# GpSimd substitution on 16x16 blocks with a 16-to-32 step on TensorE, and grouped beta/alpha products

## The chip, the cores and the metric

One core of a Trainium2 chip runs the program. The metric is device time in microseconds (us), lower is better. The kernel before takes 2449.17 us, the median of three runs (2448.19 to 2454.17).

## The reference

Two layers of a hybrid block act on 384 tokens: 128 context tokens and 256 latent tokens, 2048 channels wide. In each layer one input projection feeds two branches. Branch A is a 31-tap depthwise convolution with a LayerNorm. Branch B is a bidirectional gated DeltaNet with 8 heads of 128 channels. For a chunk of tokens, a head and a direction it solves a unit-triangular system:

```
beta = sigmoid(beta_l)                     # 8 heads x 2 directions a token
g    = -exp(a_log) * softplus(alpha_l + dt_bias)
a    = einsum(kb, k) * decay               # kb = k * beta
a    = where(strict, a, 0.0) + eye(CHUNK)  # unit lower triangular
u    = triangular_solve(a, v * beta)
w    = triangular_solve(a, kb * exp(g))
```

`beta_l` and `alpha_l` are 32 columns of the input projection. The branches are gated, merged and projected back, and a residual is added.

## The kernel before

Activations lie channel by token: tiles of 128 channels by 384 tokens. Weights stream in halves of 8 blocks of 128x128 (512 KB, tile `w`). ScalarE rounds a half to `whi`, VectorE (for some halves GpSimd) subtracts to get `wlo`, and TensorE forms three 384-column products for each block (`mm3`, line 332): `whi` by the high part of the activation, `whi` by its low part, `wlo` by the high part. These main products write `pm`. Every tensor instruction of a kind is recorded at one helper line: products at line 148, VectorE and GpSimd arithmetic at 177, DMAs at 201, ScalarE at 137.

The order on every engine is written at build time by a planner (lines 75 to 210) that books a cost for each instruction and keeps a clock for each engine. `slot` (line 403) issues one quarter of a main job, 12 products, after which generators waiting for "p" may put small products on TensorE; generators in phase "v" put VectorE and ScalarE work ahead of the next slot. The convolution (`conv31`, `t<-px,par,t` in the rows) is filler: it goes onto VectorE until VectorE's booked clock has reached TensorE's. Engines run their queues in order.

A layer has these stages in the profiled execution. First the opening: normalised tiles `hn[k]`, k = 0 to 15, are made, and the first jobs and the beta/alpha product run (`ba_mm`, line 643: 32 weight columns by the 384 columns of a float32 tile `h`, one product for each k at column group 32*(k % 4), written to `px`). Then the head stage: 40 main jobs for q, k, v and the convolution's inputs, among which the 8 heads run as generators. Then wide main products only.

A head's `invert` (line 813) solves two directions by three blocks of 128 tokens, six systems (`NI`). From each it takes the four diagonal 32x32 blocks into `dg`, writes them to DRAM (`dd`) and reads them back as 24 partitions of 32x32 (`ax`). GpSimd inverts them by substitution: 31 steps, each an outer product into `o` and a subtraction from `ax` (lines 830 to 836). The result goes through DRAM (`dx`) into `xc`, with four DMAs where rows change partitions. VectorE spreads it to `x64` and `xt64`; TensorE then builds 64x64 and 128x128 inverses in four groups of small products (`ypf`/`ypb`, `xf`/`xb`, `y2p`, `x2p`, tiles `h`). `head_out` applies the result. `free` (line 839) holds the generator until TensorE's booked clock has reached the end booked for `dx`.

The SP queue issues the weight loads and all the DMAs named but `dx`, which is GpSimd's.

Of the kernel before, what the change touches and what calls it, by code (L numbers as in the profile page):

```python
# [52 lines left out]
for _n, _w in PAR:  # L53
# [1 line left out]
    _o += _w  # L55
NPAR = _o

CST = [("ident", 128), ("mask_f", 128), ("mask_b", 128), ("xmask", 64),
       ("ones", 128), ("sel32", 32), ("sel2", 2)]
CST_OFF = {}  # L60
_o = 0
# [7 lines left out]
def hybrid_step_kernel(ctx: ExitStack, tc: tile.TileContext, x_in, cvec, w_mod, w_modt, w_first, w_in, w_ba,  # L69
# [351 lines left out]
    def mod_job(l, cs):  # L421

        w = []

        def load(n):
            for a in ((0, 3, 6), (9, 12, 15))[n]:
                b = min(a + 3, KT)
                t = t2([P, 3, 2, P])
                dma(out=t[:, 0:b - a], in_=w_mod[cs[0]][:, a:b])
                w.append(t)  # L430

        def run():
            v = pg([P, 2, P])
            for q in range(2):
                def mms(q=q):
                    for k in range(8 * q, 8 * q + 8):
                        g = 32 * (k % 4)
                        mm_(v[g:g + 32], csil[:, k, :], w[k // 3][:, k % 3], start=(k < 4), stop=(k >= 12))
                slot(last_half[0], mms)
            live[0] -= 6  # L440
            spawn(finish(v))

        def finish(v):
            vs = t1([P, 2, P])
# [13 lines left out]
            while "v" not in rs_x:  # L458
                yield
            h = make_hn(l, k)  # L460
            live[0] += 1 - (k % 2)
            yield "p"
            ba_mm(k, h)
            hn_done.add(k)

        return {"w": w, "load": [lambda n=n: load(n) for n in range(2)], "run": run}
# [161 lines left out]
    def make_hn(l, k, lo_eng=ptt):  # L628

        if k == 0:  # L630
            if l:
                load_ba(l)
            ba["ps"] = px([P, NTOK])
        u, h = t1(), t1()
        for s, sl in ((0, CTX), (1, LAT)):
            stt(out=u[:, sl], in0=xt[k][:, sl], scalar=amul[l][:, k, s:s + 1], in1=rs_x["v"][:, sl],
                op0=ALU.mult, op1=ALU.mult)
            act(h[:, sl], u[:, sl], AF.Identity, bias=modt[l][:, k, s:s + 1])
        hn[k] = t2([P, 2, NTOK], F32R)
        split(hn[k], h, False, lo_eng)  # L640
        return h

    def ba_mm(k, h):
        g = 32 * (k % 4)
        mm_(ba["ps"][g:g + 32, :], ba["w"][:, k, :], h, start=(k < 4), stop=(k >= 12))

    gd = {}

# [164 lines left out]
    def invert(l, hd):  # L813
# [9 lines left out]
        dd = dram.tile([P, NI, 32], F32, tag="dd", name="dd", bufs=2)  # L823
        dma(out=dd, in_=dg.rearrange("p d b i -> p (d b) i"))
        yield 2
        ax = sub.tile([4 * NI, 32, 32], F32, tag="ax", name="ax", bufs=NA)
        for q in range(4):
            dma(out=ax[NI * q:NI * q + NI], in_=dd[32 * q:32 * q + 32].rearrange("j n i -> n j i"))
        pset(out=ax.rearrange("p i j -> p (i j)")[:, 0:1024:33], value=1.0)
        for j in range(31):  # L830
            n, m = 31 - j, j + 1
            o = sub.tile([4 * NI, 256], F32, tag="o", name="o", bufs=1)
            ov = o[:, 0:n * m].rearrange("p (r c) -> p r c", r=n)
            ptt(out=ov, in0=ax[:, j, j + 1:32].unsqueeze(2).to_broadcast([4 * NI, n, m]),
                                    in1=ax[:, j, 0:m].unsqueeze(1).to_broadcast([4 * NI, n, m]), op=ALU.mult)
            ptt(out=ax[:, j + 1:32, 0:m], in0=ax[:, j + 1:32, 0:m], in1=ov, op=ALU.subtract)
        dx = dram.tile([4 * NI, 32, 32], F32, tag="dx", name="dx", bufs=2)
        dma(out=dx, in_=ax, q="pool")
        free = last[0]
        while clock["pe"] < free:  # L840
# [9 lines left out]
        xc = t1([P, NI, 32])  # L850
        for q in range(4):
            dma(out=xc[32 * q:32 * q + 32], in_=dx[NI * q:NI * q + NI].rearrange("n i c -> i n c"))
        yield 2
        x64, xt64 = h1([P, NI, 64]), h1([P, NI, 64])
        tt(out=x64.rearrange("p n (e c) -> p n e c", e=2), in0=xc.unsqueeze(2).to_broadcast([P, NI, 2, 32]),
           in1=C("xmask").rearrange("p (e c) -> p e c", e=2).unsqueeze(1).to_broadcast([P, NI, 2, 32]), op=ALU.mult)
        vtrans(out=xt64.rearrange("p n (e c) -> p (n e) c", e=2), in_=x64.rearrange("p n (e c) -> p (n e) c", e=2))
        yield "p"
# [167 lines left out]
    def layer(l):  # L1026
# [244 lines left out]
            return f  # L1271


        hk = {}

        def open_layer():
            del rs_x["v"]
            yield from rows_task()
            for a in range(HNA):
                hk[a] = make_hn(l, a, tt)  # L1280
            st["open"] = True


        def first_half(i):
            def run(hs, at):
                if i == 0:
                    st["acc"] = [pm(), pm(), pm(), pg([P, NTOK])]
                for q in range(2):
                    k = 2 * i + q
                    if l == 0:  # L1290
                        settle(lambda: k in hn_done)
                    else:
                        settle(lambda: "open" in st)
                        if k + HNA < KT:
                            hk[k + HNA] = make_hn(l, k + HNA)

                    def mms(k=k, q=q, h=hk.pop(k) if l else None):
                        if l:
                            ba_mm(k, h)
# [227 lines left out]
def _consts():  # L1527
# [10 lines left out]
    put("xmask", (e == q % 2) & (cc <= i[:, None] % 32))  # L1538
# [92 lines left out]
```

## Time and profile before

| what | value |
|---|---|
| median of three runs | 2449.17 us |
| the profiled execution's own time | 2447.77 us |
| its span | 2446.0 us |
| TensorE (PE) busy | 2330.2 us, 95% |
| VectorE (DVE) busy | 1835.7 us, 75% |
| ScalarE (ACT) busy | 951.6 us, 39% |
| GpSimd (POOL) busy | 869.1 us, 36% |
| head stage of layer 0, of layer 1 | 190 to 690 us, 1322 to 1830 us |

Products overlap in TensorE's pipeline, so the length of one is longer than the distance from one to the next; the distance between starts is what it costs. A float32 product stands as two records. The time of 2447.77 us is the span and 1.77 us around it.

### The profile page before, as it was taken

Reading aid. Unit: us, or ns where it says so; the run is one execution under the profiler, and the core shown is the slowest. Engines: PE = TensorE matmul, PEld = TensorE weight load, DVE = VectorE, ACT = ScalarE, POOL = GpSimd, SP = SyncE. Lnnn points to the kernel's source line nnn. Section 1 sums busy time; section 2 is a strip of 40 time slices with the busy share of each in tenths; the row PEclk is TensorE's granted clock in tenths of the full one; section 3 lists DMA queues with packets and bytes.
Section 4 is the critical chain, followed back from the end, with each engine's and each line's share of the span. In section 5 each row is a group of like instructions: output and inputs, shape, how many; then the busy total and the mean of one; then the engine's idle time right before and its main releaser. Section 6 shows DMA issues by size and latency. Waiting matters only on the chain.

```text
span 2446.0 us, 40033 instructions
## 1 busy us (share of the span) xinstructions
PE 2330.2 (95%) x14727; PEld 2237.6 (91%) x14727; DVE 1835.7 (75%) x4223; ACT 951.6 (39%) x1823; POOL 869.1 (36%) x1192
## 2 busy tenths in 40 slices
PE   6999989989989999999999999999989999999997
PEld 4789988989979999999998998988889999999997
DVE  3447989989875599899977999999975489333533
ACT  4224444444454222223344444444454322222432
POOL 1120688667630111111242188756670011110212
PEclk9999999999999999999999999999999999999998
DMA  9874433333323688787853433333333477333443
GB/s 340 287 257 149 137 107 99 111 104 104 98 91 109 206 269 265 255 266 259 310 160 104 130 114 108 108 104 113 95 103 114 152 254 239 130 125 132 137 158 111
DMA packets 163269, 398.26 MB, mean 163 GB/s; under 512 B 40960, under 2 KB 70752, under 8 KB 163072
## 3 DMA queue, kind: packets, MB, share of 16 engines
q1 hardware_dynamic: 159376, 387.66, 48.9%
q0 software_dynamic: 2176, 5.90, 0.7%
q8 instruction: 116, 1.90, 0.3%
q10 hardware_dynamic: 1520, 2.13, 0.2%
q14 instruction: 81, 0.66, 0.1%
HBM read 379.72 MB, written 15.91 MB: 162 GB/s over the span
## 4 chain that ended last, share of the span: by engine, by line
PE 64%; DVE 19%; POOL 7%; DMA 3%; issue 3%; ACT 3%; SPq 1%; DVEq 0%; ACTq 0%; POOLq 0%
PE pm L148 54%; DVE t L177 10%; PE pg L148 8%; DVE wlo L177 4%; POOL ax L177 4%; POOL o L177 3%; ACT t L137 2%; DVE h L177 1%; DMA t<-in_w_mod_dram 1%; PE px L148 1%; ACT jk L137 1%; DVE rk0t L177 1%; PE pg L152 1%; SPq L201 1%; DMA w<-in_w_in_dram 1%
## 5 line engine op out<-in xcount | busy, mean ns | idle before, releaser
L148 PE MATMUL pm<-t,whi 128*128 128x384 f32 x7264 | 1903.6, 343 | 5.8 <-ACT whi L137 5.8
L148 PEld LDWEIGHTS pm<-t,whi 128*128 128x128 f32 x7264 | 1314.5, 190 | 26.8 <-ACT whi L137 7.4
L148 PE MATMUL pm<-t,wlo 128*128 128x384 f32 x3632 | 1232.6, 339 | 31.1 <-DVE wlo L177 31.1
L177 DVE TENSOR_TENSOR wlo<-w,whi 128x1024 fp32r<-128x1024 f32 x453 | 587.5, 1298 | 207.3 <-ACT whi L137 206.2
L148 PEld LDWEIGHTS pm<-t,wlo 128*128 128x128 f32 x3632 | 688.2, 189 | 38.1 <-DVE wlo L177 37.9
L137 ACT ACTIVATE whi<-w 128x1024 fp32r<-128x1024 f32 x480 | 505.2, 1054 | 383.0 <-PE pm L148 301.1
L177 POOL TENSOR_TENSOR ax<-ax,o 24x31 f32<-24x31 f32 (+15 forms) x496 | 332.4, 670 | 38.9
L137 ACT ACTIVATE t<-t 128x384 f32<-128x384 f32 (+5 forms) x299 | 137.7, 467 | 525.4 <-DVE t L177 479.9
L177 POOL TENSOR_TENSOR o<-ax 24x31 f32<-24x31 f32 (+15 forms) x496 | 309.4, 624 | 38.9
L177 DVE SCALAR_TENSOR_TENSOR t<-px,par,t 128x113 f32<-128x113 f32 (+26 forms) x768 | 248.7, 367 | 12.0 <-ACT px L137 6.9
L177 POOL TENSOR_TENSOR t<-t,t 128x384 fp32r<-128x384 f32 (+2 forms) x66 | 88.0, 1337 | 383.0 <-DVE t L177 305.4
L177 POOL TENSOR_TENSOR wlo<-w,whi 128x1024 fp32r<-128x1024 f32 x27 | 65.0, 2408 | 433.0 <-ACT whi L137 421.1
L177 DVE SCALAR_TENSOR_TENSOR px<-wm,pg 128x512 f32<-128x512 f32 x256 | 177.1, 692 | 8.7 <-DMA wm<-in_w_modt_dram 5.3
L177 DVE SCALAR_TENSOR_TENSOR wm<-wm,pg 128x512 f32<-128x512 f32 x256 | 167.2, 681 | 7.3 <-PE pg L152 7.3
L137 ACT ACTIVATE t<-pm 128x384 f32<-128x384 f32 x122 | 56.1, 488 | 176.1 <-PE pm L148 175.9
L148 PE MATMUL pg<-t,whi 128*128 128x384 f32 (+1 forms) x416 | 110.9, 348 | 3.3 <-ACT h L137 1.2
L189 POOL MEMSET ax<- 24x32 f32 x16 | 2.5, 158 | 270.7 <-DMA ax<-dd 270.7
L177 DVE TENSOR_TENSOR t<-t,t 128x384 f32<-128x384 f32 (+1 forms) x122 | 81.6, 679 | 22.1 <-ACT t L137 20.9
L177 DVE SCALAR_TENSOR_TENSOR t<-t,t 128x384 f32<-128x384 f32 x96 | 60.0, 625 | 44.1 <-ACT t L137 43.8
L177 POOL TENSOR_TENSOR accx<-accx,t 128x384 f32<-128x384 f32 x28 | 29.6, 1057 | 174.9 <-ACT t L137 146.9
L148 PEld LDWEIGHTS pg<-t,whi 128*128 128x128 f32 x416 | 74.9, 191 | 12.9 <-issue 4.5
L177 POOL TENSOR_TENSOR h<-h,t 128x384 f32<-128x384 f32 x16 | 16.3, 1017 | 172.4 <-DVE t L177 172.4
(152 smaller groups left out, 1683.3 us busy)
## 6 DMA issues: line engine op xcount, KB each, us to landing
w<-in_w_in_dram SPq DMA_DIRECT2D x318, 512.0 KB
wm<-in_w_modt_dram SPq DMA_DIRECT2D x128, 512.0 KB
w<-in_w_p_dram SPq DMA_DIRECT2D x64, 512.0 KB
w<-in_w_o_dram SPq DMA_DIRECT2D x64, 512.0 KB
t<-in_w_mod_dram SPq DMA_DIRECT2D x80, 384.0 KB
w<-in_w_first_dram SPq DMA_DIRECT2D x16, 512.0 KB
t<-in_x_dram SPq DMA_DIRECT2D x16, 384.0 KB
t<-gdram SPq DMA_DIRECT2D x16, 384.0 KB
```

Of the source, the lines that this page charges most:

```text
L137: return nc.scalar.activation(out, in_, func, **k)
L148: return nc.tensor.matmul(out, lhsT, rhs, start=start, stop=stop)
L152: nc.tensor.transpose(out, in_, ident)
L177: return f(**k)
L189: pset = vec(lambda out, value: nc.gpsimd.memset(out, value), 1e-3, "pool", 0.05)
L201: eng.dma_start(out=out, in_=in_)
```

## The change

The substitution works on 16x16 blocks: 48 partitions, 15 steps. `dg` is folded so that each partition keeps the 16 columns of its own diagonal block (`dc`, with the constant `hsel`). The blocks go out to `dd`, in to `ax`, out to `dx` and in to `xc` with one DMA each instead of one, four, one and four. The step from 16 to 32 is new on TensorE: VectorE spreads `xc` to `x32` and transposes it, 24 products of 32x32 by 16 columns make `ypf` and `ypb`, both are copied to `y32`, 24 more make `xp`, and one VectorE operation adds it into `x32`. From `x64` on the head is as before.

`ba_mm` no longer takes `h`. It runs only at k = 3, 7, 11 and 15, and then issues eight products: for each of the two parts of `hn`, four products at the four column groups.

```
 def ba_mm(k):
+    if k % 4 < 3:
+        return
+    for half in range(2):
+        for i in range(k - 3, k + 1):
+            g = 32 * (i % 4)
+            mm_(ba["ps"][g:g + 32, :], ba["w"][:, i, :], hn[i][:, half, :].bitcast(F32),
+                start=(i < 4 and half == 0), stop=(i >= 12 and half == 1))
...
-        dma(out=dd, in_=dg.rearrange("p d b i -> p (d b) i"))
+        dc, df = t1([P, NI, 16]), dg.rearrange("p d b i -> p (d b) i")
+        act(dc, df[:, :, 0:16], AF.Copy, scale=C("hsel")[:, 0:1])
+        stt(out=dc, in0=df[:, :, 16:32], scalar=C("hsel")[:, 1:2], in1=dc, op0=ALU.mult, op1=ALU.add)
+        yield
+        dma(out=dd.rearrange("n p j -> p n j"), in_=dc)
...
-        for q in range(4):
-            dma(out=ax[NI * q:NI * q + NI], in_=dd[32 * q:32 * q + 32].rearrange("j n i -> n j i"))
-        for j in range(31):
-            n, m = 31 - j, j + 1
+        dma(out=ax, in_=dd.rearrange("n (g i) j -> (n g) i j", g=8))
+        for j in range(15):
+            n, m = 15 - j, j + 1
...
-        for q in range(4):
-            dma(out=xc[32 * q:32 * q + 32], in_=dx[NI * q:NI * q + NI].rearrange("n i c -> i n c"))
+        dma(out=xc, in_=dx.rearrange("(n g) i c -> (g i) n c", g=8))
         yield 2
+        tt(out=x32..., in0=xc..., in1=C("hmask")..., op=ALU.mult)
+        vtrans(out=xt32, in_=x32)
+        vset(out=y32[:, NF:, 0:16], value=0.0)
+        yield "p"
+        ypf, ypb = pg([P, NF, 16]), pg([P, NF, 16])
+        for n in range(NF):
+            for q in range(4):
+                mm_(ypf[g, n, :], ap[0][g, n, 0, g], x32[g, n, 0:16], start=True, stop=True)
+            for q in range(4):
+                mm_(ypb[g, n, :], ap[1][g, n, 0, g], xt32[g, NF + n, 16:32], start=True, stop=True)
+        yield
+        vcopy(out=y32[:, 0:NF, 0:16], in_=ypf)
+        act(y32[:, NF:, 16:32], ypb, AF.Copy)
+        yield "p"
+        xp = pg([P, NI, 16])
...
+        stt(out=x32[:, :, 0:16], in0=xp, scalar=C("lowneg"), in1=x32[:, :, 0:16], op0=ALU.mult, op1=ALU.add)
```

In the order of TensorE, at the first head of layer 0, the kernel before goes from the main products straight to `ypf`/`ypb` of the 32-to-64 step (`h_3374` is `x64`, `h_3375` is `xt64`):

```order
L148 MATMUL pm<-t_919,whi 128x384 x2
L148 MATMUL pm<-t_919,wlo 128x384
L148 MATMUL pg<-h_3374,t_2421 64x32
L148 MATMUL pg<-h_3375,t_2422 64x32
...
L148 MATMUL pg<-t_3075 128x256
L148 MATMUL pm<-t_1032,whi 128x384 x2
```

The changed kernel has two more groups there (`h_3029` holds `x32` and `y32`, `t_3030` is `xt32`, `h_3129` is `x64`):

```order
L148 MATMUL pm<-t_920,whi 128x384 x2
L148 MATMUL pm<-t_920,wlo 128x384
L148 MATMUL pg<-h_3029,t_2437 32x16 x4
L148 MATMUL pg<-t_3030,t_2438 32x16 x4
...
L148 MATMUL pm<-t_1046,whi 128x384 x2
L148 MATMUL pm<-t_1046,wlo 128x384
...
L148 MATMUL pg<-h_3029,t_3030 32x16 x4
L148 MATMUL pg<-h_3029 32x16 x4
...
L148 MATMUL pm<-t_1403,whi 128x384 x2
L148 MATMUL pg<-h_3129,t_2437 64x32
```

Each of the two groups has 24 products and stands in a gap between main products that had none; 12 main products lie between them.

On TensorE in the opening of layer 1, the kernel before has one beta/alpha product ahead of the 12 main products of each k:

```order
L148 MATMUL pg<-t_13317,wlo 128x386
L148 MATMUL px<-t_13471,t_13467 32x384
L148 MATMUL pm<-t_13476,whi 128x384 x2
L148 MATMUL pm<-t_13476,wlo 128x384
...
L148 MATMUL pg<-t_13476,wlo 128x384
L148 MATMUL px<-t_13480,t_13467 32x384
L148 MATMUL pm<-t_13485,whi 128x384 x2
```

The changed kernel has eight in a row at every fourth k (the four `hn` tiles, first part, then the same four again):

```order
L148 MATMUL pg<-t_13668,wlo 128x384
L148 MATMUL px<-t_13556,t_13547 32x384
L148 MATMUL px<-t_13565,t_13547 32x384
L148 MATMUL px<-t_13668,t_13547 32x384
L148 MATMUL px<-t_13692,t_13547 32x384
...
L148 MATMUL pm<-t_13692,whi 128x384 x2
L148 MATMUL pm<-t_13692,wlo 128x384
```

Sixteen interruptions of the main products become four.

On VectorE at the first head of layer 0, the changed kernel has the spreading of `xc` (`t_2935`) ahead of a weight half's `wlo`:

```order
L177 SCALAR_TENSOR_TENSOR t_3004<-pm,par_93,t_3004 128x255
L177 TENSOR_TENSOR h_3029<-t_2935,cst 128x192
L177 STREAM_TRANSPOSE t_3030<-h_3029 128x192
L184 MEMSET h_3029 128x3x16
L177 SCALAR_TENSOR_TENSOR t_3003<-t_3015,t_3004 128x3x128
L177 TENSOR_TENSOR wlo<-w_2837,whi 128x1024
```

In the kernel before the operations that read the blocks stood like this:

```order
L177 SCALAR_TENSOR_TENSOR t_3296<-t_3201,G,cst 128x128 x3
L177 TENSOR_TENSOR h_3374<-t_3330,cst 128x384
L177 STREAM_TRANSPOSE h_3375<-h_3374 128x384
L177 SCALAR_TENSOR_TENSOR t_1971<-px,par_93,t_1971 128x113
L177 SCALAR_TENSOR_TENSOR t_1971<-px,par_93,t_1971 128x114
L177 TENSOR_TENSOR wlo<-w_3187,whi 128x1024
```

In both a weight half stands behind the operation that waits for the blocks' DMA; the operation itself is half as wide now, and `x64` follows later as well.

## Rows read from the trace of the kernel before

**Rows 1.** The page's first part: busy time of each engine.

```profile
PE 2330.2 (95%) x14727; PEld 2237.6 (91%) x14727; DVE 1835.7 (75%) x4223; ACT 951.6 (39%) x1823; POOL 869.1 (36%) x1192
```

**Rows 2.** Busy by stage: stretch, length, then PE, PEld, DVE, ACT, POOL, PEclk, DMA, GB/s.

```profile
60.00:190.00 130.00, 128.61 (x954) 103.56 (x953) 59.66 (x123) 37.17 (x61) 27.29 (x27) 1.00 0.79 264
190.00:690.00 500.00, 464.48 (x3178) 447.50 (x3176) 451.14 (x1147) 221.78 (x532) 321.99 (x505) 0.98 0.36 112
765.00:1250.00 485.00, 485.00 (x2787) 484.52 (x2784) 422.04 (x998) 157.87 (x206) 75.58 (x54) 1.00 0.74 247
1250.00:1322.00 72.00, 72.00 (x361) 57.96 (x361) 50.88 (x76) 32.38 (x62) 31.50 (x24) 1.00 0.43 132
1322.00:1830.00 508.00, 475.59 (x3224) 456.36 (x3223) 468.25 (x1177) 236.57 (x555) 327.26 (x512) 0.97 0.35 109
```

**Rows 3.** What PE waited for, whole span: total us, times, longest.

```profile
PE pm L148 <- DVE wlo L177: 31.1, 21, 7.8
PE pg L148 <- DVE h L177: 12.2, 17, 5.9
```

**Rows 4.** Timeline of PE around a head's `ypf`/`ypb` group: start, length, instruction.

```profile
711.36 0.34 PE L148 MATMUL pm<-t,wlo 128*128 128x384 f32 x1
711.62 0.55 PE L148 MATMUL pg<-h,t 32*64 32x32 f32 x24
712.10 0.61 PE L148 MATMUL pm<-t,whi 128*128 128x384 f32 x2
712.56 0.33 PE L148 MATMUL pm<-t,wlo 128*128 128x384 f32 x1
```

**Rows 5.** Timeline of PE in layer 1's opening: two beta/alpha products that follow each other.

```profile
1272.69 0.83 PE L148 MATMUL px<-t,t 128*32 128x384 f32 x2
...
1275.74 0.83 PE L148 MATMUL px<-t,t 128*32 128x384 f32 x2
```

**Rows 6.** Timeline of PE in layer 0's opening: modulation products at four column groups.

```profile
60.63 2.80 PE L148 MATMUL pg<-t,csil 128*32 128x256 f32 x48
```

**Rows 7.** Costliest groups of the page: GpSimd's substitution, busy, mean ns.

```profile
L177 POOL TENSOR_TENSOR ax<-ax,o 24x31 f32<-24x31 f32 (+15 forms) x496 | 332.4, 670 | 38.9
...
L177 POOL TENSOR_TENSOR o<-ax 24x31 f32<-24x31 f32 (+15 forms) x496 | 309.4, 624 | 38.9
```

**Rows 8.** Timeline of POOL at the first head's first steps.

```profile
258.24 0.23 POOL L177 TENSOR_TENSOR o<-ax 24x31 f32<-24x31 f32 x1
258.54 0.26 POOL L177 TENSOR_TENSOR ax<-ax,o 24x31 f32<-24x31 f32 x1
258.88 0.28 POOL L177 TENSOR_TENSOR o<-ax 24x60 f32<-24x60 f32 x1
```

**Rows 9.** VectorE by form, 256 to 690 us: count, busy, mean ns, idle before.

```profile
L177 DVE TENSOR_TENSOR wlo<-w,whi 128x1024 fp32r<-128x1024 f32 x72 | 98.4, 1370 | 0.4
L177 DVE SCALAR_TENSOR_TENSOR t<-t,G,cst 128x128 f32<-128x128 f32 x42 | 21.7, 569 | 0.0
...
L177 DVE SCALAR_TENSOR_TENSOR rk0t<-rk0t,rk 128x3 f32<-128x3 f32 x14 | 4.2, 297 | 0.5
```

**Rows 10.** The same forms, 190 to 256 us.

```profile
L177 DVE TENSOR_TENSOR wlo<-w,whi 128x1024 fp32r<-128x1024 f32 x14 | 17.0, 1221 | 3.2 <-ACT whi L137 3.1
...
L177 DVE SCALAR_TENSOR_TENSOR t<-t,G,cst 128x128 f32<-128x128 f32 x6 | 1.7, 344 | 0.0
...
L177 DVE SCALAR_TENSOR_TENSOR rk0t<-rk0t,rk 128x3 f32<-128x3 f32 x2 | 0.3, 164 | 0.1
```

**Rows 11.** VectorE by form, 696.5 to 765 us: operations like those added.

```profile
L177 DVE TENSOR_TENSOR h<-t,cst 128x384 f32<-128x384 f32 x1 | 0.6, 551 | 0.0
...
L177 DVE TENSOR_TENSOR h<-h,pg 128x96 f32<-128x96 f32 x2 | 0.4, 240 | 0.0
```

**Rows 12.** Waits for the blocks' DMAs, whole span, VectorE's.

```profile
DVE h L177 <- DMA t<-dx: 11.0, 4, 6.9
```

**Rows 13.** Waits of the SP queue, whole span.

```profile
SPq L201 <- DMA dx<-ax: 36.1, 9, 10.1
```

More of the change, by code (lines that the diff above doesn't have):

```diff
@@ L459, in finish @@
                 yield
-            h = make_hn(l, k)
+            make_hn(l, k)
             live[0] += 1 - (k % 2)
             yield "p"
-            ba_mm(k, h)
+            ba_mm(k)
             hn_done.add(k)
@@ L640, in make_hn, with ba_mm @@
         split(hn[k], h, False, lo_eng)
[L641 to L645, printed above, removed]
+    def ba_mm(k):
+        if k % 4 < 3:
[5 more added lines that the diff above has]
+                    start=(i < 4 and half == 0), stop=(i >= 12 and half == 1))
     gd = {}
@@ L822, in invert @@
         yield
-        dd = dram.tile([P, NI, 32], F32, tag="dd", name="dd", bufs=2)
-        dma(out=dd, in_=dg.rearrange("p d b i -> p (d b) i"))
-        yield 2
-        ax = sub.tile([4 * NI, 32, 32], F32, tag="ax", name="ax", bufs=NA)
-        for q in range(4):
-            dma(out=ax[NI * q:NI * q + NI], in_=dd[32 * q:32 * q + 32].rearrange("j n i -> n j i"))
-        pset(out=ax.rearrange("p i j -> p (i j)")[:, 0:1024:33], value=1.0)
-        for j in range(31):
-            n, m = 31 - j, j + 1
-            o = sub.tile([4 * NI, 256], F32, tag="o", name="o", bufs=1)
+        dc, df = t1([P, NI, 16]), dg.rearrange("p d b i -> p (d b) i")
+        act(dc, df[:, :, 0:16], AF.Copy, scale=C("hsel")[:, 0:1])
+        stt(out=dc, in0=df[:, :, 16:32], scalar=C("hsel")[:, 1:2], in1=dc, op0=ALU.mult, op1=ALU.add)
+        yield
+        dd = dram.tile([NI, P, 16], F32, tag="dd", name="dd", bufs=2)
+        dma(out=dd.rearrange("n p j -> p n j"), in_=dc)
+        yield 2
+        NS = 8 * NI
+        ax = sub.tile([NS, 16, 16], F32, tag="ax", name="ax", bufs=NA)
+        dma(out=ax, in_=dd.rearrange("n (g i) j -> (n g) i j", g=8))
+        pset(out=ax.rearrange("p i j -> p (i j)")[:, 0:256:17], value=1.0)
+        for j in range(15):
+            n, m = 15 - j, j + 1
+            o = sub.tile([NS, 64], F32, tag="o", name="o", bufs=1)
             ov = o[:, 0:n * m].rearrange("p (r c) -> p r c", r=n)
[L834 to L837, printed above, removed]
+            ptt(out=ov, in0=ax[:, j, j + 1:16].unsqueeze(2).to_broadcast([NS, n, m]),
+                in1=ax[:, j, 0:m].unsqueeze(1).to_broadcast([NS, n, m]), op=ALU.mult)
+            ptt(out=ax[:, j + 1:16, 0:m], in0=ax[:, j + 1:16, 0:m], in1=ov, op=ALU.subtract)
+        dx = dram.tile([NS, 16, 16], F32, tag="dx", name="dx", bufs=2)
         dma(out=dx, in_=ax, q="pool")
@@ L849, in invert, with diag @@
         vset(out=U[1][0:64, :, 64:128], value=0.0)
-        xc = t1([P, NI, 32])
-        for q in range(4):
-            dma(out=xc[32 * q:32 * q + 32], in_=dx[NI * q:NI * q + NI].rearrange("n i c -> i n c"))
+        xc = t1([P, NI, 16])
+        dma(out=xc, in_=dx.rearrange("(n g) i c -> (g i) n c", g=8))
         yield 2
+        xy = h1([P, 2, NI, 32])
+        x32, y32 = xy[:, 0], xy[:, 1]
+        xt32 = t1([P, NI, 32])
+        tt(out=x32.rearrange("p n (e c) -> p n e c", e=2), in0=xc.unsqueeze(2).to_broadcast([P, NI, 2, 16]),
+           in1=C("hmask").rearrange("p (e c) -> p e c", e=2).unsqueeze(1).to_broadcast([P, NI, 2, 16]), op=ALU.mult)
+        vtrans(out=xt32, in_=x32)
+        vset(out=y32[:, NF:, 0:16], value=0.0)
+        yield "p"
+        def diag(q):
+            return slice(32 * q, 32 * q + 32)
+        ypf, ypb = pg([P, NF, 16]), pg([P, NF, 16])
+        for n in range(NF):
+            for q in range(4):
+                g = diag(q)
+                mm_(ypf[g, n, :], ap[0][g, n, 0, g], x32[g, n, 0:16], start=True, stop=True)
+            for q in range(4):
+                g = diag(q)
+                mm_(ypb[g, n, :], ap[1][g, n, 0, g], xt32[g, NF + n, 16:32], start=True, stop=True)
[4 more added lines that the diff above has]
+        xp = pg([P, NI, 16])
+        for n in range(NF):
+            for q in range(4):
+                g = diag(q)
+                mm_(xp[g, n, :], xt32[g, n, :], y32[g, n, 0:16], start=True, stop=True)
+            for q in range(4):
+                g = diag(q)
+                mm_(xp[g, NF + n, :], y32[g, NF + n, :], x32[g, NF + n, 0:16], start=True, stop=True)
+        yield
+        stt(out=x32[:, :, 0:16], in0=xp, scalar=C("lowneg"), in1=x32[:, :, 0:16], op0=ALU.mult, op1=ALU.add)
         x64, xt64 = h1([P, NI, 64]), h1([P, NI, 64])
-        tt(out=x64.rearrange("p n (e c) -> p n e c", e=2), in0=xc.unsqueeze(2).to_broadcast([P, NI, 2, 32]),
+        tt(out=x64.rearrange("p n (e c) -> p n e c", e=2), in0=x32.unsqueeze(2).to_broadcast([P, NI, 2, 32]),
            in1=C("xmask").rearrange("p (e c) -> p e c", e=2).unsqueeze(1).to_broadcast([P, NI, 2, 32]), op=ALU.mult)
@@ L1537, in _consts @@
     q, e, cc = i[:, None] // 32, np.arange(64)[None] // 32, np.arange(64)[None] % 32
-    put("xmask", (e == q % 2) & (cc <= i[:, None] % 32))
+    put("xmask", e == q % 2)
+    e, cc = np.arange(32)[None] // 16, np.arange(32)[None] % 16
+    put("hmask", (e == i[:, None] // 16 % 2) & (cc <= i[:, None] % 16))
+    put("lowneg", -1.0 * (i[:, None] % 32 >= 16))
+    put("hsel", np.arange(2)[None] == i[:, None] // 16 % 2)
     put("mask_f", np.where(i[:, None] <= i[None, :], 0.0, NEG))
```

11 lines of the change are left out of this document (5 added, 6 removed).

## The prediction

> **What bounds the kernel now.** I read the busy times first, then the busy times by stage, then the waits, and last the timeline around single groups. TensorE is busy 95% of the span and VectorE 75% [rows 1], but these are averages over different stages. In the wide stage from 765 to 1250 us TensorE is busy in all 485 us, with 2787 products: one starts every 485/2787 = 0.174 us [rows 2]. Nothing but fewer or shorter products helps there, and the change touches none of them. In the two head stages TensorE is idle for 500 - 464.5 = 35.5 us and 508 - 475.6 = 32.4 us, 68 us together, its granted clock has a mean of 0.98 and 0.97, and VectorE is busy 451 of 500 and 468 of 508 us [rows 2]. The largest waits of TensorE were ended by VectorE: 31.1 us for `wlo`, 12.2 us for the small tiles `h` [rows 3]. So in the head stages two engines are close to full, and TensorE, which has the most to do, stumbles when VectorE is late. GpSimd's long substitution (322 and 327 us of those stages [rows 2], (332.4 + 309.4)/16 = 40.1 us a head [rows 7]) is not itself what TensorE waits for.
>
> The sum below is made against the profiled execution, 2447.8 us; the median of the runs shown is 1.4 us above it, and I add these at the end.
>
> **The grouped beta/alpha products.** From one `px` product to the next takes 1275.74 - 1272.69 = 3.05 us [rows 5], of which the 12 main products explain 12 x 0.174 = 2.09. One product costs TensorE 0.96 us, sixteen 15.4 us a layer. The eight of the new form go round four column groups, as the modulation products of layer 0 do: 48 records of 256 columns in 2.80 us, 0.058 each [rows 6]. At 384 columns that is 0.087, for 16 records 1.4 us, and I add 0.3 for the interruption: 1.7 a group, 6.8 a layer, a gain of 8.6. In layer 1's opening TensorE is busy 72 of 72 us and DMA only 0.43, so all of it counts; in layer 0's it is busy 128.6 of 130 us, but DMA is at 0.79 [rows 2] and may hold it back: between 0 and 8.6, and I take 6. Term: -15 us, bounds -6 and -17. `h` was a buffer of seven and comes free earlier; as no stage of the opening shows TensorE waiting, that is worth nothing.
>
> **The 16-to-32 step on TensorE.** Two groups of 24 products a head, 32 groups in all, each in a new gap between main products. No row shows products of 32x32 by 16 columns. The nearest is the `ypf`/`ypb` group: 24 records of 32 columns, two abreast. From the main product ahead of it at 711.36 to the second one behind it at 712.56 [rows 4] is 1.20 us where three main products need 0.52: the group costs 0.68 us. The new group has twice the records with half the columns, and its four diagonal blocks share neither rows nor columns of the array, so four may run abreast. Above, if neither helps, it costs twice that, 1.36; below, if both count in full, about half, 0.34. I take the row itself, 0.68: 32 x 0.68 = +22 us, bounds +11 and +44. All of it lies on the path, since TensorE has no other slack in these stages than its waits.
>
> The Trainium skill, in "TensorEngine Tiling (Array Packing)", section Instruction Overhead, speaks against this part: it gives each matmul about 60 cycles, so that one column costs as much as sixty. By that figure, at 2.4 GHz, the 48 records would take an estimated 1.2 us one by one and the 32 groups 38 us, which would put the total near 2438. The row of 24 records in 0.48 us up to the next product [rows 4], 20 ns a record with 32 columns, does not contradict it, since a record there may already be at that floor.
>
> **GpSimd and VectorE.** The substitution goes from 62 operations of 31 to 256 elements to 30 of 15 to 64. Steps of 31 and 60 elements start 0.30 and 0.34 us apart [rows 8], so 30 take about 10 us, and with stretched ones 12, against some 45 with the gaps between them. That is off TensorE's path. What counts is VectorE: the same operations take longer while GpSimd works. Up to 256 us, before the first substitution step at 258.24, `wlo` takes 1221 ns, the decay operation 344, a three-column operation 164 [rows 10]; after that 1370, 569 and 297 [rows 9]. Over the seven heads in that stretch this is 72 x 0.149 = 10.7, 42 x 0.225 = 9.5, and for about 25 three- and six-column operations a head 25 x 7 x 0.133 = 23 us: 43, or 6.2 a head, 99 for sixteen. With a quarter of the GpSimd time left, three quarters of it goes: -73 us. Added on VectorE for each head are two operations of half the width of the 551 ns one, some 0.30 us each, two narrow ones near 0.24 [rows 11], and a copy and a memset, together about 1.3 us: +21 in all. VectorE loses 52 us of its 919 in the two stages.
>
> How much of this reaches TensorE no row shows directly. Of its 68 idle us VectorE ended 43 [rows 3]. Bounds: nothing, and all 68. I take three quarters of the 43, the share by which the interference falls: -32 us. The 32 new groups each wait for a fresh small copy; the planner leaves these a slot of 12 main products, so I take +4 us, bounds 0 and +16. The clock's loss, 2% of 500 and 3% of 508, is 25 us [rows 2]; if it falls with the stalls, a quarter of it comes back: -6, bounds 0 and -15.
>
> **DMAs.** Six fewer for each head, at the SP queue. That queue waited 36.1 us for `dx` in 9 places [rows 13] and VectorE 11.0 us in 4 for the blocks [rows 12], small beside 1008 us of head stages. The pieces of `dd` and `xc` shrink to 64 bytes; a slower landing lengthens a head that has become some 30 us shorter. I book zero. The cover is the planner's `free` and the two slots behind it; what it costs if they fall short is the second rival. ScalarE gets two small operations more for each head at 222 of 500 us busy [rows 2]: zero.
>
> Sum: -15 + 22 - 32 + 4 - 6 = -27. 2447.8 - 27 + 1.4 = 2422 us.
>
> **Rivals.**
> First, the small groups cost double. Records of 16 columns cost what those of 32 do and do not run four abreast: 44 us instead of 22, total 2444, no change that can be told. For it: twice the records of the measured group. Against: `csil` records overlap four abreast [rows 6].
>
> Second, the blocks come late and VectorE, which works in order, stops ahead of a `wlo` half: the spreading of `xc` now stands directly before conv and `wlo` work on which the next main products wait. The planner books about 10 us for a substitution that takes about 12, and 64-byte pieces may add to it. If each of 16 heads held VectorE for 4 us, and two thirds of that reached TensorE (of VectorE's longest such wait, 6.9 us [rows 12], TensorE's longest for `h`, 5.9 us [rows 3], is most), that is +43: 2465, slower. It decides from 27/(16 x 0.67) = 2.5 us a head. Against: only 4 of 16 heads waited for blocks before, 11.0 us in total [rows 12], with a substitution four times as long to misjudge.
>
> Third, VectorE's lateness stood behind nearly all idle time, ScalarE's late evictions too: three quarters of 68, and half the clock's loss: -15 + 22 - 51 - 12 = -56, 2393.
>
> Fourth, the eight products do not overlap, as the parts of `hn` write the same columns again: 8 x 0.96 for what cost 4 x 0.96, +31 instead of -15: 2468. Against it stand 0.087 against 0.48 us a record [rows 5, 6].
>
> **How the numbers follow.** I give the forecast 0.60, the first rival 0.17, the second 0.09, the third 0.11, the fourth 0.03. The measurement can tell 0.3%, 7 us, from no change. Faster: nearly all of the forecast, 0.57, the third, 0.11, and a part of the first, 0.05, make 0.73. Within: the rest of the first, 0.12, and of the forecast, 0.03: 0.15. Slower: the second and fourth, 0.12. The range reaches down to the third rival and a little past it, 2388, and up past the first to where the second begins, 2452; it leaves out most of the second and fourth and the unknown bounds' far ends.
>
> **What would show it.** Right: a beta/alpha group near 1.7 us between main products in layer 1; the `x32`/`xp` groups near 0.7 us; `wlo` in the head stages near 1260 ns and three-column operations near 190; GpSimd busy near 85 us in each head stage; TensorE's idle time there near 40 us in all. Wrong: groups at 1.3 us; a wait of VectorE for `xc` in most heads; idle time that stays at 68 us although `wlo` got shorter, which would mean that the planned order and not VectorE's pace makes the stalls.

## The result and the profile after

The changed kernel takes 2396.3 us, the median of four runs (2392.86 to 2398.55), against 2449.3 for the kernel before: a ratio of 0.9779 with a 95% interval of 0.976 to 0.9797, or 53 us less. The forecast was 2422 with a range of 2388 to 2452. So the direction and the range held, and the gain is twice the forecast 27 us: the time lies near the third rival's 2393, not near the forecast. The profiled execution took 2394.9 us.

The first part of the page after answers to [rows 1]. VectorE's busy time fell by 73 us, GpSimd's by more than half, TensorE's by only 14:

```profile
PE 2316.3 (97%) x16327; PEld 2239.7 (94%) x16327; DVE 1762.8 (74%) x4319; ACT 960.5 (40%) x1855; POOL 398.6 (17%) x680
```

To compare stages, both traces have to be cut where the same main product starts, since the later stages have moved. First the kernel before, cut in this way: the opening and the head stage of layer 0, then those of layer 1. The columns are those of [rows 2]: stretch, length, busy time of PE, PEld, DVE, ACT and POOL, granted clock, DMA share, GB/s.

```profile
65.50:192.40 126.90, 125.51 (x896) 102.96 (x893) 59.88 (x120) 36.31 (x58) 26.73 (x28) 1.00 0.79 265
192.40:690.50 498.10, 462.58 (x3169) 445.60 (x3168) 450.10 (x1145) 222.28 (x532) 321.63 (x505) 0.98 0.36 111
1250.20:1322.00 71.80, 71.80 (x360) 57.76 (x360) 50.68 (x76) 32.18 (x62) 31.30 (x24) 1.00 0.43 133
...
1322.00:1830.10 508.10, 475.69 (x3224) 456.46 (x3223) 468.35 (x1177) 236.61 (x555) 327.26 (x512) 0.97 0.35 109
```

The same four stretches of the changed kernel:

```profile
64.00:184.90 120.90, 118.92 (x920) 103.08 (x917) 60.72 (x120) 36.28 (x58) 25.14 (x28) 1.00 0.81 279
184.90:660.50 475.60, 465.61 (x3941) 448.18 (x3939) 419.58 (x1215) 229.49 (x558) 90.37 (x258) 0.99 0.37 114
...
1216.00:1286.10 70.10, 66.78 (x392) 57.86 (x391) 50.97 (x76) 32.20 (x62) 31.13 (x24) 1.00 0.39 129
1286.10:1777.80 491.70, 478.07 (x4031) 460.31 (x4031) 431.35 (x1232) 239.88 (x576) 95.35 (x256) 0.99 0.36 109
```

The two head stages together went from 1006.2 to 967.3 us (-38.9), although TensorE is busy 5.4 us longer in them: its idle time fell from 67.9 to 23.6 us. The openings gave 6.0 and 1.7 us. The stretch behind layer 0's heads (690.5 to 765.1 before, 660.5 to 730.4 after) gave 4.7, the wide stages nothing. The start of the first stretch, 64.0 to 68.4 us in the kernels below, moves by some us from run to run with nothing changed ahead of it.

The waits of TensorE that answer to [rows 3], and one that the prediction did not name (GpSimd's low part of `hn`):

```profile
PE pm L148 <- DVE wlo L177: 10.7, 9, 2.2
...
PE pg L148 <- DVE h L177: 6.7, 15, 1.3
...
PE pm L148 <- POOL t L177: 3.2, 7, 0.9
```

VectorE by form in the head stage of layer 0 (250 to 655 us: count, busy, mean ns), beside [rows 9, 10]:

```profile
L177 DVE TENSOR_TENSOR wlo<-w,whi 128x1024 fp32r<-128x1024 f32 x72 | 88.0, 1222 | 0.5 <-ACT whi L137 0.4
L177 DVE SCALAR_TENSOR_TENSOR t<-t,G,cst 128x128 f32<-128x128 f32 x42 | 12.0, 342 | 0.0
...
L177 DVE SCALAR_TENSOR_TENSOR rk0t<-rk0t,rk 128x3 f32<-128x3 f32 x12 | 1.9, 162 | 0.4
```

These are the undisturbed lengths of [rows 10] (1221, 344, 164 ns), not the forecast 1260 and 190: the interference went nearly altogether, not by three quarters. GpSimd's substitution, on the page after, beside [rows 7]:

```profile
L177 POOL TENSOR_TENSOR o<-ax 48x15 f32<-48x15 f32 (+7 forms) x240 | 87.5, 365 | 19.0 <-POOL ax L189 0.2
...
L177 POOL TENSOR_TENSOR ax<-ax,o 48x15 f32<-48x15 f32 (+7 forms) x240 | 86.3, 360 | 18.8
```

That is 10.9 us a head instead of 40.1, 27% of what it was. Last, TensorE around the first new group of one head:

```profile
482.02 0.34 PE L148 MATMUL pm<-t,wlo 128*128 128x384 f32 x1
482.29 0.25 PE L148 MATMUL pg<-h,t 32*32 32x16 f32 x8
...
482.66 0.23 PE L148 MATMUL pg<-t,t 32*32 32x16 f32 x6
482.82 0.55 PE L152 MATMUL pg<-cst,t 128*128 128x128 f32 x3
```

From the main product ahead at 482.02 to the next instruction behind the group at 482.82 is 0.80 us, less 0.17 for the main product: 0.63, against the forecast 0.68 from [rows 4]. By their starts in the trace, 18 of the 32 groups take the same; most of the others hold a wait.

### The profile page after: what moved, and what is told of

Its sections match the earlier page's. It is cut to its first block, busy times and chain, and to the rows that moved or that the text cites. A ratio compares the mean times of both kernels' runs of the same rounds, so it can differ in the third digit from the quotient of the medians.

```text
span 2393.1 us, 42725 instructions
## 1 busy us (share of the span) xinstructions
PE 2316.3 (97%) x16327; PEld 2239.7 (94%) x16327; DVE 1762.8 (74%) x4319; ACT 960.5 (40%) x1855; POOL 398.6 (17%) x680
## 5 line engine op out<-in xcount | busy, mean ns | idle before, releaser
L148 PE MATMUL pm<-t,wlo 128*128 128x384 f32 x3632 | 1228.6, 338 | 11.3 <-DVE wlo L177 10.7
L177 DVE TENSOR_TENSOR wlo<-w,whi 128x1024 fp32r<-128x1024 f32 x453 | 567.7, 1255 | 202.3 <-ACT whi L137 200.9
L177 POOL TENSOR_TENSOR wlo<-w,whi 128x1024 fp32r<-128x1024 f32 x27 | 64.9, 2404 | 486.0 <-ACT whi L137 474.1
L177 DVE TENSOR_TENSOR t<-t,t 128x384 f32<-128x384 f32 (+1 forms) x122 | 73.2, 610 | 25.7 <-ACT t L137 24.6
L177 POOL TENSOR_TENSOR o<-ax 48x15 f32<-48x15 f32 (+7 forms) x240 | 87.5, 365 | 19.0 <-POOL ax L189 0.2
L177 DVE SCALAR_TENSOR_TENSOR t<-t,t 128x384 f32<-128x384 f32 x96 | 53.1, 554 | 49.5 <-ACT t L137 49.0
L177 POOL TENSOR_TENSOR ax<-ax,o 48x15 f32<-48x15 f32 (+7 forms) x240 | 86.3, 360 | 18.8
L148 PE MATMUL pg<-t,wlo 128*128 128x384 f32 (+1 forms) x208 | 70.7, 340 | 0.0
L137 ACT ACTIVATE t<-pg 128x384 f32<-128x384 f32 (+5 forms) x91 | 34.3, 383 | 88.9 <-PE pg L148 77.9
```

The costliest lines, as they stand in the source:

```text
L137: return nc.scalar.activation(out, in_, func, **k)
L148: return nc.tensor.matmul(out, lhsT, rhs, start=start, stop=stop)
L177: return f(**k)
```

## The experiments

Each ratio is to the kernel before (2449 to 2452 us in these sessions), with its 95% interval; one hundredth is 24.5 us. "Heads" is the length of the two head stages together, cut at the same main products, from the one trace of each kernel. That one execution can lie off the median: it took 4 us more than the median for short GpSimd, 5 for the step issued twice and 5.5 for the three copies. The time lost to TensorE's lower clock level differs between traces by several us as well.

| kernel | us | ratio | heads, us |
|---|---|---|---|
| before | 2449.3 | 1 | 1006.2 |
| changed | 2396.3 | 0.9779 (0.976 to 0.9797) | 967.3 |
| beta/alpha grouping alone | 2437.6 | 0.9948 (0.9933 to 0.9962) | 1002.5 |
| substitution and step alone | 2408.8 | 0.9827 (0.9814 to 0.984) | 968.4 |
| short GpSimd | 2363.7 | 0.965 (0.9637 to 0.9664) | 926.8 |
| the same, left-out steps behind the store | 2448.2 | 0.999 (0.9982 to 0.9999) | 1000.0 |
| short GpSimd, with the step's VectorE part | 2387.8 | 0.9745 (0.973 to 0.9759) | 943.8 |
| changed, further GpSimd work | 2459.9 | 1.0042 (1.0029 to 1.0054) | 1032.8 |
| changed, step issued twice | 2408.3 | 0.9824 (0.9806 to 0.9842) | 983.3 |
| changed, DMAs in four | 2403.3 | 0.9802 (0.9788 to 0.9815) | 973.7 |
| changed, low parts on VectorE | 2392.1 | 0.9759 (0.9746 to 0.9773) | 965.9 |
| the same, three copies on ScalarE | 2389.5 | 0.9754 (0.9738 to 0.9771) | 971.9 |

### Short GpSimd: the relief alone

```
-        for j in range(31):
-            ptt(...); ptt(...)
+        for j in range(31):          # the planner books all 31
+            f = ptt if j < 5 or j >= 25 else skip
+            f(...); f(...)
```

> The kernel before with 11 of the 31 steps of the substitution issued (the first 5 and the last 6; the 20 between them are booked by the planner but left out, so the blocks are not inverted fully): the planned order of all engines is that of before, GpSimd is busy a third as long, no step on TensorE is added, all DMAs stay. Relief of VectorE alone: if the head stages' idle time of TensorE falls as in the changed kernel (46 us) and the clock rises with it, and the TensorE step costs 22 us in the changed kernel: 2449 - 60 to 70 = 2380 to 2390. If the step costs only 11: 2449 - 55 = 2394. If the relief is the forecast three quarters of 43, 32 + 6: 2411. If idle time in these stages is set by the planned order and not by VectorE's pace: 2449.

Measured 2363.7, a gain of 86 us, more than any theory gave. The two head stages of this kernel:

```profile
191.20:645.80 454.60, 450.35 (x3169) 437.52 (x3168) 408.38 (x1146) 223.14 (x534) 89.22 (x195) 1.00 0.39 121
1277.10:1749.30 472.20, 462.96 (x3223) 447.33 (x3223) 424.06 (x1178) 236.72 (x555) 93.04 (x192) 1.00 0.38 117
```

With TensorE's order of before, its idle time is 4.3 and 9.2 us instead of 35.5 and 32.4, and the clock is at 1.00. VectorE is busy 832.4 us instead of 918.5, 86 less; the stages are 79.4 shorter, nine tenths of that, in an execution 4 us above the median. GpSimd does nothing else in layer 0's head stage but issue the stores `dx` and `gpart`. No wait of TensorE or VectorE there is put down to GpSimd, and VectorE's wait for `gpart` over the whole span did not fall (8.5 us before, 11.3 here), so GpSimd's own lateness is not what was relieved. But this kernel also hands over a head's blocks some 30 us earlier. The next one tells the two apart.

### The left-out steps behind the store

```
         dma(out=dx, in_=ax, q="pool")
+        for j in range(5, 25):
+            nc.gpsimd.tensor_tensor(out=ov, ...); nc.gpsimd.tensor_tensor(out=ax[...], ...)
```

> The short-GpSimd kernel (the kernel before with 11 of 31 steps ahead of the store of dx), with the 20 left-out steps issued behind that store instead, on the same tile: GpSimd does the same 62 operations a head as before, but the blocks leave it after 11 steps, so the chain of a head is as short as in the short-GpSimd kernel (its output is again not the reference's, since the stored blocks are not inverted fully). The planned order of all engines is that of before. If the gain in the head stages is VectorE set free from GpSimd's work: nearly all of it goes, 2435 to 2449, wlo back near 1370 ns. If it is the shorter chain of a head (blocks that come early): 2364 to 2370 stays. In between if both count: 2400.

Measured 2448.2: the whole gain of 86 us is gone, although a head's blocks leave GpSimd after as few steps as in the kernel above, and VectorE waits only 2.7 us in 2 places for the blocks, instead of 11.0 in 4. Its head stages:

```profile
195.30:685.70 490.40, 459.42 (x3168) 442.45 (x3167) 451.17 (x1144) 220.62 (x531) 312.86 (x504) 0.98 0.37 113
1318.80:1828.40 509.60, 475.72 (x3225) 455.91 (x3224) 466.99 (x1178) 235.92 (x555) 329.64 (x512) 0.98 0.36 108
```

VectorE's forms in it, 258 to 685 us:

```profile
L177 DVE TENSOR_TENSOR wlo<-w,whi 128x1024 fp32r<-128x1024 f32 x72 | 98.4, 1369 | 0.3
L177 DVE SCALAR_TENSOR_TENSOR t<-t,G,cst 128x128 f32<-128x128 f32 x42 | 23.8, 619 | 0.0
L177 DVE SCALAR_TENSOR_TENSOR rk0t<-rk0t,rk 128x3 f32<-128x3 f32 x14 | 4.0, 287 | 0.5
```

`wlo` is back at 1369 ns, VectorE at 918.2 us and TensorE's idle time at 64.9. GpSimd's operations beside VectorE's are the cause; the shorter chain of a head, with these operations in place, is worth at most the 6 us by which the head stages are shorter than before.

### The step's VectorE part

```
 (short GpSimd, and at the places of the step, on scratch columns of tiles already held:)
+        activation(z, ...); scalar_tensor_tensor(z, ...)                  # at dc
+        tensor_tensor(z, ...); transpose(z, z); memset(z, ...)            # behind xc
+        tensor_copy(z, ...); activation(z, ...); scalar_tensor_tensor(z, ...)
```

> The short-GpSimd kernel (its output is not the reference's, the blocks are not inverted fully) with the small operations that the 16-to-32 step adds on VectorE (six a head) and ScalarE (two a head), issued on scratch data, without the step's 48 matmuls. The step as a whole costs 2409 - 2364 = 45 us over that kernel. If the matmuls and their interruptions are its price (the prediction's 22, and its waits 4) and VectorE's 1.3 us a head the rest: 2364 + 15 to 21 = 2379 to 2385. If VectorE has room for the small operations now that GpSimd does not hold it up: 2364 to 2369, and the remaining 20 us lie in the waits that the new groups bring.

Measured 2387.8, 23 us above the short-GpSimd kernel (0.9745 against 0.965), a little more than the theory that VectorE's work counts. Its head stages:

```profile
195.00:654.70 459.70, 453.29 (x3169) 438.98 (x3167) 417.02 (x1189) 226.58 (x549) 90.73 (x195) 1.00 0.39 120
1286.40:1770.50 484.10, 467.32 (x3224) 449.92 (x3224) 434.24 (x1226) 240.17 (x571) 90.24 (x192) 0.99 0.37 114
```

VectorE is busy 18.8 us longer and the stages are 17.0 longer: nine tenths again, with the other sign.

### The substitution and the step without the grouping

```
-    def ba_mm(k):                          # eight products at k = 3, 7, 11, 15
+    def ba_mm(k, h):                       # one product for each k, of h
```

> The changed kernel with the beta/alpha products one by one again; the 16x16 substitution and the 16-to-32 step on TensorE stay. If the two parts add up and the head stages gave 44 us and the openings 8.5: 2405, TensorE idle in the head stages as low as in the changed kernel (near 29 us). If the beta/alpha edit is worth the predicted 15: 2411. If the freed buffers of the edit (h comes free earlier) helped the head stages too: 2410 or more with more idle time of TensorE there.

Measured 2408.8 (0.9827). Its interval (0.9814 to 0.984 of 2450, 2404 to 2411) holds both the 2405 of the two traces and the prediction's 2411, so the run does not decide between them. The third theory falls: TensorE's idle time in the head stages is 25.0 us, as low as in the changed kernel (23.6). Its head stages:

```profile
194.80:672.50 477.70, 466.29 (x3941) 448.73 (x3939) 419.19 (x1215) 229.58 (x558) 90.94 (x259) 0.99 0.38 114
1300.40:1791.10 490.70, 477.13 (x4030) 458.85 (x4030) 430.54 (x1232) 239.86 (x576) 95.36 (x256) 0.99 0.36 109
```

They are 968.4 us long, 24.6 more than with the step's VectorE part alone: the price of 32 groups on TensorE with their waits (22 and 4 in the prediction), less what the fewer DMAs of this kernel give; its substitution and the planned order differ as well. TensorE's busy time has risen by 22.8 of these, its idle time by 1.8. The stretch behind layer 0's heads is 4.6 us shorter than there, so over the program the difference is 20 us (0.9827 against 0.9745).

### The step issued twice

```
         for n in range(NF):
             for q in range(4):
                 mm_(ypf[g, n, :], ...)
...
+        (the 24 products once more, unbooked, behind the first 24; the same for xp)
```

> The changed kernel with every product of the 16-to-32 step issued twice in a row (the same values written again), in the same place and with nothing else moved: 32 groups become twice as long, without a new interruption. By the prediction's row a group costs 0.68 us, of which a part is the interruption and is not paid again: at most +22, 2418. If records of 16 columns run four abreast and count half: +5 to +11, 2401 to 2407. If they cost double (first rival): +44, 2440.

Measured 2408.3: 12 us more. The group shown above for the changed kernel, issued twice:

```profile
488.58 0.34 PE L148 MATMUL pm<-t,wlo 128*128 128x384 f32 x1
488.85 0.25 PE L148 MATMUL pg<-h,t 32*32 32x16 f32 x8
...
489.77 0.55 PE L152 MATMUL pg<-cst,t 128*128 128x128 f32 x3
```

It takes 489.77 - 488.58 = 1.19 us instead of 0.80, so 24 further products (48 records) cost 0.39; by their starts, 22 of the 32 groups show 0.38 to 0.40. That is 8 ns a record, where the first issue with its interruption takes 0.63 us. For 32 groups it makes some 12.5 us, as measured; the head stages of this trace are 16.0 longer, with 5 us more lost to the lower clock level than in the changed kernel's trace. So about a third of the price of a small group is the interruption of the main products, and twice the records does not mean twice the cost. The first rival falls, by the 0.63 us itself. The figure of the Trainium skill that the prediction weighed, "TensorEngine Tiling (Array Packing)", section Instruction Overhead, about 60 cycles for a matmul, or an estimated 25 ns at 2.4 GHz, is not seen one after another here: these products stand at four diagonal blocks of the array, and the measured 8 ns a record, or 17 ns a product, decide.

### Further GpSimd work in the changed kernel

```
         dma(out=dx, in_=ax, q="pool")
+        nc.gpsimd.memset(zx, 0.0)
+        for j in range(23):                # a 24x24 substitution on scratch
+            nc.gpsimd.tensor_tensor(out=zv, ...); nc.gpsimd.tensor_tensor(out=zx[...], ...)
```

> The changed kernel with 46 further GpSimd operations a head on scratch data (a memset and 23 steps of a 24x24 substitution), issued behind the store of dx, so that no head waits for them and the planned order of all engines is the same: GpSimd is busy about as long as before the change, the chain of a head stays short, and the TensorE step stays. If the gain of the head stages is the interference of GpSimd with VectorE, it goes: wlo back near 1370 ns there, the three-column operations near 300, TensorE's idle time in the head stages back from 29 us to 60 or more, and 2396 + 40 to 50 = 2436 to 2446. If it is the shorter chain and the fewer DMAs of a head: 2396 to 2400.

Measured 2459.9, 63 us slower than the changed kernel, more than expected, but the experiment has a flaw: a layer's second substitution starts 21 us behind the first in the changed kernel, and here it queued behind the added work. The timeline of the second head (start, length, engine, instruction, idle time and what ended it):

```profile
304.51 0.71 PE L148 MATMUL pg<-vpp,t 128*128 128x128 f32 x4
311.71 0.56 POOL L201 DMA_DIRECT2D dx<-ax  x1 [0.29 <-POOL ax L177]
314.40 0.38 SPq L201 DMA_DIRECT2D t<-dx  x1
...
316.40 0.36 DVE L177 TENSOR_TENSOR h<-t,cst 128x192 f32<-128x192 f32 x1 [14.60 <-DMA t<-dx]
...
316.90 0.30 PE L148 MATMUL pg<-h,t 32*32 32x16 f32 x8 [11.68 <-DVE h L177]
```

VectorE stands for 14.6 us before `xc`, with the conv and `wlo` work of the next main products behind it, and TensorE for 11.7 and soon for 5.9 more; layer 1 has 16.3 and 6.6 us there. These 40 us are the second rival's mechanism at its full price, brought on by the experiment and not by the change. The other 23 us, found by subtraction alone, are put down to interference: VectorE is busy 892.3 us in the head stages instead of 850.9. It is weaker than before, `wlo` at 1261 ns instead of 1370, though GpSimd is busy 541 of the 649 us of before in the head stages: the added operations have 144 elements at most, those of before 256.

### The grouping alone

```
 def ba_mm(k):
+    if k % 4 < 3:
+        return
+    (eight products; before with nothing else changed)
```

> The kernel before with the grouped beta/alpha products alone; the substitution stays as it was. By the prediction's term both openings gain, 8.6 us in layer 1 and 6 in layer 0: 2449 - 15 = 2434. By the theory formed from the two traces, that layer 1's opening is now paced by the supply of hn (VectorE, ScalarE, VectorE, GpSimd in turn, about 3.1 us for one k, as long as TensorE took before), only layer 0's opening gains, 7.5 us, and layer 1's 1 us: 2440 to 2441, with waits of TensorE for GpSimd's low parts in layer 1's opening. If the openings' difference in the changed kernel came from something other than this edit: 2449.

Measured 2437.6: 12.7 us (9 to 16), near the prediction's 15. But its openings, cut as above, are these:

```profile
66.90:187.90 121.00, 119.02 (x920) 103.15 (x917) 60.71 (x120) 36.29 (x58) 25.16 (x28) 1.00 0.82 276
1243.50:1313.60 70.10, 66.85 (x393) 57.95 (x393) 50.98 (x76) 32.30 (x62) 31.07 (x24) 1.00 0.43 129
```

Layer 0's gains 5.9 us and layer 1's 1.7, as in the changed kernel; the head stages are 3.7 us shorter and the stretch behind layer 0's heads is 1.4 longer. What remains of the 12.7 is not settled; the start of the first stretch alone moves by more.

### The low parts of layer 1's opening on VectorE

```
-                            make_hn(l, k + HNA)
+                            make_hn(l, k + HNA, tt)
```

> The changed kernel with the low parts of hn in layer 1's opening computed on VectorE and not on GpSimd (14 subtractions of 128x384 move; nothing else is edited). If the supply of hn paces this opening since the beta/alpha products are grouped, and GpSimd's 1.49 us with the stretch it puts on VectorE's operations is what makes it slow: TensorE's waits for the low parts go and the opening gains up to the 8 us that the prediction expected of it, 2389. If VectorE becomes the bound instead: no gain or a loss, 2396 to 2405. If the supply does not pace the opening: 2396.

The opening went from 70.1 to 67.5 us, by its row (the columns are those of the stages above):

```profile
1219.60:1287.10 67.50, 65.34 (x392) 57.47 (x391) 48.13 (x90) 32.38 (x62) 10.71 (x10) 1.00 0.40 130
```

VectorE's two operations on `amul` in this opening, in the changed kernel:

```profile
L177 DVE SCALAR_TENSOR_TENSOR t<-t,amul,t 128x256 f32<-128x256 f32 x16 | 13.7, 858 | 0.0
L177 DVE SCALAR_TENSOR_TENSOR t<-t,amul,t 128x128 f32<-128x128 f32 x16 | 11.7, 732 | 0.8 <-ACT t L137 0.8
```

The same operations with the low parts on VectorE:

```profile
L177 DVE SCALAR_TENSOR_TENSOR t<-t,amul,t 128x256 f32<-128x256 f32 x16 | 7.6, 478 | 0.0
L177 DVE SCALAR_TENSOR_TENSOR t<-t,amul,t 128x128 f32<-128x128 f32 x16 | 7.1, 447 | 0.8 <-ACT t L137 0.8
```

VectorE took over 14 subtractions (7.8 us) and is yet busy 2.8 us less, since its own operations beside GpSimd's had been stretched from 478 to 858 ns. The supply of `hn` did hold TensorE, but only 2.6 of the missing 7 us come back. The total, 2392.1 against 2396.3, is a gain by the stage and not by the overlapping intervals.

### Three copies on ScalarE

```
 (with the low parts on VectorE)
-        vcopy(out=y32[:, 0:NF, 0:16], in_=ypf)
+        act(y32[:, 0:NF, 0:16], ypf, AF.Copy)
...
-        vcopy(out=U[0][lo, :, 0:64], in_=xt64[lo, 0:NF, :])     # and U[1]
+        act(U[0][lo, :, 0:64], xt64[lo, 0:NF, :], AF.Copy)
```

> The changed kernel with the low parts of layer 1's opening on VectorE, and in the head stages three copies a head moved from VectorE to ScalarE (the one of the new step's product, and two ahead of the last block product). If VectorE's load still paces TensorE in the head stages: 2 to 6 us faster than the low parts alone (2392), 2386 to 2390. If what is left there are the new groups and their waits on TensorE: 2391 to 2394.

Measured 2389.5, not distinct from 2392.1. VectorE lost only 6 us in the head stages, which became 6 us longer in an execution 5.5 us above the median; 5 of the 6 are the lower clock level, and 4.5 us were gained in the stretch behind layer 0's heads. The planner's order moves with the copies. This run shows no effect of VectorE's load either way.

### The DMAs in four again

```
-        dma(out=ax, in_=dd...)                 -        dma(out=xc, in_=dx...)
+        dma(out=ax, in_=dd..., parts_=4)       +        dma(out=xc, in_=dx..., parts_=4)
```

> The changed kernel with the two DMAs that read the blocks of a head (the spread into ax and the spread into xc) split in four each again, as before: six more DMAs a head, the same bytes and pieces, the planner's bookings unchanged. By the prediction, which books the DMAs at nothing: 2396, within 3 us. If the fewer DMAs gave a part of the head stages' gain (the queue that feeds the weights is held, or the head's chain is longer): slower by 10 us or more, with VectorE or GpSimd waiting longer for ax and xc.

Measured 2403.3 (0.9802 against 0.9779; the intervals overlap), the head stages 6.4 us longer. VectorE's wait for the blocks in the changed kernel (total, times, longest):

```profile
DVE h L177 <- DMA t<-dx: 10.8, 7, 2.4
```

The same wait with the DMAs in four:

```profile
DVE h L177 <- DMA t<-dx: 20.8, 9, 3.4
```

So the six fewer DMAs a head are likely worth some 6 us, and the prediction's zero was low.

## Why the prediction came out too small

**The 16-to-32 step on TensorE: right.** 32 groups at 0.68 us, +22, and +4 for their waits; measured 0.63 us for one, and 24.6 in the head stages, or some 31 if the fewer DMAs hide 6 of them.

**VectorE's own gain: nearly right.** Forecast -73 for the interference and +21 for the new operations; measured -86 (short GpSimd) and +18.8, together the -67.5 by which VectorE's busy time in these stages fell with the change. The step that was off is "With a quarter of the GpSimd time left, three quarters of it goes". Interference does not go with GpSimd's busy time. By the starts and lengths in the traces of layer 0's head stage, 801 VectorE operations ran beside a GpSimd one before and lost 58 ns each against the same forms alone, 47 us in all, near the 50 that the forecast 99 for both layers implies. After the change it is 287, and 6 ns each. It is not that the short substitution falls on other work: conv operations, which read PSUM and are not stretched, are 44% of these operations before and 47% after. But of the 48 decay operations 42 met GpSimd before and none after, and of the 56 `rk0t` operations 42 and none; the `wlo` that still meet it lose some 40 ns, where they lost some 200. And what they meet has at most 64 elements instead of 256; which of these counts most is open.

The Trainium skill, "SBUF — State Buffer", section Who interferes with whom, has a rule for this: a VectorE instruction with two SBUF inputs contends with a GpSimd instruction that reads SBUF; with at most one SBUF input, outside its two-port modes, it doesn't contend. The rows agree: `rk0t` with two such inputs took 297 ns and now takes 162, while a conv operation with a PSUM input is the same. In the kernel before it took 336 ns:

```profile
L177 DVE SCALAR_TENSOR_TENSOR t<-px,par,t 128x127 f32<-128x127 f32 x14 | 4.7, 336 | 0.0
```

And in the changed kernel 339 ns:

```profile
L177 DVE SCALAR_TENSOR_TENSOR t<-px,par,t 128x127 f32<-128x127 f32 x14 | 4.7, 339 | 0.0
```

**What reaches TensorE: the step that failed.** "Of its 68 idle us VectorE ended 43 ... I take three quarters of the 43": -32, and -6 for the clock. The relief alone gave 79.4 us in the head stages, of which 54.4 are idle time. Another 22.2 are clock: by the traces' clock records the head stages of before lose 25.6 us at the lower of the two levels (1.2 instead of 2.4 GHz), those with the short substitution 3.4. One such stretch of before starts at 501.6 us, while TensorE waits 7.8 us for `wlo`. The last 2.8 us are closer products. The waits put down to VectorE were not the limit (40 of the 43 us lie in the head stages; [rows 3] are of the whole span). The kernel before also waited for ScalarE's eviction `vpp`:

```profile
PE pg L148 <- ACT vpp L137: 9.2, 4, 3.1
```

That wait is in neither the changed kernel's list nor the short-GpSimd kernel's, and it stands at 9.6 us where the steps come back behind the store. In the two head stages TensorE's idle time before divides into 44.4 us put down to VectorE and 22.7 to ScalarE; with the short substitution it is 10.8 and 2.1, and with the steps behind the store 41.4 and 22.7 again. So ScalarE's lateness came and went with VectorE's, one step further back. That is the third rival's thought: its -51 and -12 for idle time and clock are together near the -62.4 measured below, and its 2393 is nearer than the forecast's 2422. In place of the share: in two runs these stages moved by nine tenths of VectorE's busy time, -79.4 for -86.0 and +17.0 for +18.8. It is no constant: the further GpSimd work gave some 25 us of head stages, beside its queue, for 41.4 us of VectorE, and the three copies gave nothing for 6. At nine tenths, the prediction's own -73 + 21 would have given -47 where it put -38; the measured amounts give -62.4.

**The grouped products.** -15 forecast, -12.7 by the times. But of the 8.6 in layer 1's opening 1.7 came. Part of the mistake is the old price: by the starts in the trace before, the sixteen products of that opening cost 13.8 us, 0.86 each and not 0.96. The other part is a new wait: TensorE's busy time there fell by 5.0 us (71.80 to 66.78), but 3.3 us of idle time came, 3.2 of it for GpSimd's low parts. A group, with the product ahead and the one behind:

```profile
1245.47 0.34 PE L148 MATMUL pg<-t,wlo 128*128 128x384 f32 x1
1245.74 1.92 PE L148 MATMUL px<-t,t 128*32 128x384 f32 x16
1247.59 0.62 PE L148 MATMUL pm<-t,whi 128*128 128x384 f32 x2
```

It takes 1247.59 - 1245.47 - 0.17 = 1.95 us, near the forecast 1.7; the fourth rival (eight times 0.96) falls.

**The sum of the head stages.** Relief -79.4, VectorE's new work +17.0, the groups and their waits +24.6 with whatever the fewer DMAs give: -37.8, against -12 forecast. That difference of 26 us is the miss. With -7.7 of the openings and -4.7 behind layer 0's heads it makes 50 of the 53 us.

**The second rival** did not come to pass: VectorE's wait for the blocks is 10.8 us in 7 places, beside [rows 12], and the queue's for `dx` 48.0 us beside [rows 13].

## What to carry to other kernels

Where two engines are both near full, read the busy time of the second and not only the waits that are put down to it: a slower eviction by a third engine and a lower clock can both be its lateness at one remove. Before costing a GpSimd operation at nothing, look for VectorE operations of the same form with and without it; what they lose is a cost of GpSimd's work. An experiment that adds work behind a store must leave the engine free in time for the next user, or it measures a queue.

## What the runs showed that was not expected

GpSimd's interference falls faster than its work: 27% of the substitution time left, and 1222 against 1370 ns for `wlo`, nearly all of the loss gone. With 83% of the busy time but operations of at most 144 elements, `wlo` lost 40 of 149 ns.

A second issue of 24 small products at four diagonal blocks costs 0.39 us, some 8 ns a record, where the first with its interruption costs 0.63.

Moving 14 subtractions from GpSimd to VectorE made VectorE less busy (50.97 to 48.13 us), not more.
